# GpSimd forms the low parts of a weight tile in four operations of 256 columns instead of one of 1024

## The chip, the cores and the metric

The kernel runs on one core of one Trainium2 chip. The metric is the device time of one execution in microseconds (us). A core has TensorE (matrix products; the profile keeps its matmuls, PE, apart from its weight loads, PEld), VectorE (DVE), ScalarE (ACT), GpSimd (POOL) and SyncE (SP, which here issues DMAs).

## The reference

One encoder layer over 512 tokens of width 1024, float32:

```python
# x: (1, 512, 1024)
p = rmsnorm(x, norm1_g) @ w_in          # one combined projection
p_A, p_B, g_A, g_B = split(p)
y_A = rwkv7_bidirectional(p_A, ...)     # 8 heads of 64: a recurrence over the tokens, forwards and backwards
y_B = neighbourhood_attention_2d(p_B)   # 8 heads, tokens as an 8 x 64 grid, window of 8 x 16
x = x + (sigmoid(g_A) * (y_A @ w_oA) + sigmoid(g_B) * (y_B @ w_oB)) @ w_out
x = x + hier_moe(rmsnorm(x, norm2_g))   # 4 groups of 8 experts, top 1 group, top 2 experts in it
```

`rwkv7_bidirectional` ends in a normalisation over each head's 64 columns, and `neighbourhood_attention_2d` normalises q and k per head: both need an inverse square root for each token and head.

## The kernel before

A projection is computed in tiles of 128 output columns. The weight tile, `w_raw`, has 128 partitions by 1024 numbers: eight blocks k of 128 x 128, one for each 128 rows of the weight. TensorE multiplies rounded operands (`fp32r`), so each operand is split in two: a high part, rounded, and a low part, what is left. `proj` (L303) adds up three products for each k, low weight by high activation, high by high, and high by low, so 24 matmuls of 128x512 a tile.

`wsplit` (L294) makes the two parts of a weight tile. ScalarE writes `w_hi`, a rounded copy. Then `w_lo` = `w_raw` - `w_hi` is one subtraction over the whole tile: on VectorE for the 15 first tiles of `w_in` but one and for the later `wo` and `w_out` tiles, on GpSimd for the others of `w_in` (`m >= 15` in `proj`) and for the second tile of the kernel: 30 tiles on VectorE, 29 on GpSimd. `w_raw`, `w_hi` and `w_lo` have two buffers each. SP issues the loads of `w_raw`.

The work runs in this order. The first 15 tiles of `w_in` are RWKV's input (`rwkv_tile`). For each of two groups of heads the kernel then prepares per-chunk matrices (`prep_unit`, whose results are `T`, `KB` and the state `R`), inverts triangular blocks (`invert`: a series of small DVE operations on `pr` and `TI`, each dependent on the one before, then a 32x32 transpose into `MT`), and walks through 16 chunks one after the other (`chain_step`: products into `c`, copies to `X` and `R` by ScalarE and DVE, then the state's product with the decay `EX`, a DVE operation with PSUM input). `chain_out` normalises the result: `gx`, `gst` and `rs_i` are its small DVE operations, and `yc` is scaled by DVE for one half and by GpSimd for the other. Tiles of attention's q, k, v and of the gates (`others`) are projected in between, to fill TensorE while the chain waits; a scheduler sets the order of each engine from the dependencies and the priorities that the code gives. `na_qk` normalises q and k over `osq`; `na_block` adds the bias `BM`, formed on GpSimd, to the attention scores. From about 560 us on, the output projections and the experts follow.

Both normalisations call `rsqrt_bits`, which is a series of eleven small DVE operations, each on the result of the one before: a shift by one bit of the number's own bits (`nrs_i` in `na_qk`, `rs_i` in `chain_out`), one multiply and add on it (`nst`, `gst`), and three Newton steps of three operations.

In the profile a helper's operation has the helper's line: L188 is an activation on ScalarE, L191 a `tensor_tensor`, L194 a `scalar_tensor_tensor`, L198 and L200 a `tensor_scalar`, L203 a matmul and L206 a transpose on TensorE.

Of the kernel before, what the change touches and what calls it, by code (L numbers as in the profile page):

```python
# [8 lines left out]
F32 = mybir.dt.float32  # L9
# [4 lines left out]
OP = mybir.AluOpType  # L14
# [4 lines left out]
D = 1024  # L19
# [162 lines left out]
class K:  # L182
# [111 lines left out]
    def wsplit(self, raw, eng=None):  # L294
        hi = self.wpool.tile([P, 8, P], F32R, name="w_hi", tag="w_hi", bufs=2)
        lo = self.wpool.tile([P, 8, P], F32R, name="w_lo", tag="w_lo", bufs=2)
        self.act(hi.rearrange("p a b -> p (a b)"), raw)
        self.tt(lo.rearrange("p a b -> p (a b)"), raw, hi.rearrange("p a b -> p (a b)").bitcast(F32), OP.subtract, eng=eng)
        return hi, lo

    def wload(self, m, name="w_in", eng=None):
# [1150 lines left out]
```

## Time and profile before

| | |
|---|---|
| median of 3 runs | 927.93 us (926.7 to 929.12) |
| profiled execution | 931.2 us |
| its span on the core | 929.4 us |
| mean granted TensorE clock | 0.949 of full speed |
| TensorE matmul busy | 814.1 us, 88% of the span |
| VectorE busy | 433.4 us, 47% |
| ScalarE busy | 308.9 us, 33% |
| GpSimd busy | 181.5 us, 20%, 161 instructions |
| of this `w_lo` on GpSimd | 70.6 us, 29 tiles |

A row of the timeline gives an instruction's start in the span and its duration in us, its engine and line, the operation, the tiles (out<-in) with their shape, how many equal neighbours the row stands for, and in brackets the engine's idle time before it and what ended that. A row of a group gives the count, the busy time in us, the mean of one in ns, and the idle time before them with what ended it. A row of waits gives who waited for whom, in us, how often, and the longest.

### The profile page before, as it was taken

To read this page: it belongs to the slowest core of one execution; us is meant where nothing else is said; L and a number is where in the kernel's file an instruction comes from. 1 tells how busy PE (TensorE), PEld (TensorE's weight loads), DVE (VectorE), ACT (ScalarE), POOL (GpSimd) and SP (SyncE) were. 2 spreads that over 40 slices of the span, in tenths; PEclk is the share of its full clock that TensorE was granted. 3 is DMA by queue.
4 is the path that set the end of the run, shared out by engine and by line. 5 is a ranking of instruction groups with operands and counts; after the bars stand their busy time and mean duration, and the time that the engine had idled before them with its cause. 6 is when DMAs were issued, how large, how long until landed. Compare 5 with 4: busy or idle time off the path is not lost. (4 is left out here: it accounts for less than half of the span.)

```text
span 929.4 us, 17293 instructions
## 1 busy us (share of the span) xinstructions
PE 814.1 (88%) x7192; PEld 529.8 (57%) x7192; DVE 433.4 (47%) x870; ACT 308.9 (33%) x667; POOL 181.5 (20%) x161
## 2 busy tenths in 40 slices
PE   8999887889987987799999999999669999888784
PEld 7676555556666765566666677878533333333331
DVE  5798984565689587224436505643612111111010
ACT  6454531123433553034756722223211111111110
POOL 2611121120003142123312230003321121211010
PEclk9999996899999999599999999999779999999998
DMA  6311130212112311422224548889989999999982
GB/s 216 110 59 47 35 102 26 68 58 69 36 59 81 125 53 62 140 72 67 81 68 137 182 135 287 300 326 380 353 330 410 394 345 395 395 393 400 398 341 44
DMA packets 49263, 176.18 MB, mean 190 GB/s; under 512 B 7584, under 2 KB 14368, under 8 KB 37152
## 3 DMA queue, kind: packets, MB, share of 16 engines
q1 hardware_dynamic: 43936, 164.56, 48.1%
q0 software_dynamic: 5248, 10.50, 4.2%
q8 instruction: 57, 0.93, 0.4%
q14 instruction: 22, 0.18, 0.1%
HBM read 159.30 MB, written 24.12 MB: 197 GB/s over the span
## 5 line engine op out<-in xcount | busy, mean ns | idle before, releaser
L203 PE MATMUL G<-ws,xT 128*64 128x512 f32 x512 | 128.9, 600 | 5.1 <-DMA ws<-in_wgu 3.8
L203 PE MATMUL mm<-hT_hi,w_lo 128*128 128x512 f32 x264 | 113.9, 432 | 7.9 <-ACT oth L188 6.8
L191 POOL TENSOR_TENSOR w_lo<-w_raw,w_hi 128x1024 fp32r<-128x1024 f32 x29 | 70.6, 2436 | 237.2 <-ACT w_hi L188 213.8
L203 PE MATMUL mm<-hT_hi,w_hi 128*128 128x512 f32 x264 | 112.0, 424 | 0.0
L203 PE MATMUL mm<-hT_lo,w_hi 128*128 128x512 f32 x264 | 111.2, 421 | 0.0
L203 PEld LDWEIGHTS G<-ws,xT 128*64 128x64 f32 x512 | 44.5, 138 | 77.7 <-issue 65.3
L203 PE MATMUL Yd<-ws,hT 128*64 128x512 f32 x256 | 65.7, 606 | 9.7 <-ACT y L188 8.7
L188 ACT ACTIVATE w_hi<-w_raw 128x1024 fp32r<-128x1024 f32 x59 | 62.2, 1055 | 30.5 <-PE mm L203 29.4
L203 PEld LDWEIGHTS mm<-hT_hi,w_lo 128*128 128x128 f32 x264 | 51.9, 197 | 26.2 <-issue 15.3
L191 DVE TENSOR_TENSOR w_lo<-w_raw,w_hi 128x1024 fp32r<-128x1024 f32 x30 | 37.7, 1257 | 50.1 <-ACT w_hi L188 50.1
L203 PEld LDWEIGHTS mm<-hT_lo,w_hi 128*128 128x128 f32 x264 | 51.8, 196 | 12.7 <-issue 2.0
L203 PEld LDWEIGHTS mm<-hT_hi,w_hi 128*128 128x128 f32 x264 | 52.0, 197 | 11.3 <-issue 1.5
L191 DVE TENSOR_TENSOR sg<-sg,G 128x256 f32<-128x256 f32 x16 | 6.7, 421 | 96.9 <-ACT sg L188 96.9
L1382 POOL DMA_INDIRECT out<-y,idx x16 | 25.2, 1577 | 117.3 <-DVE y L198 100.4
L198 DVE TENSOR_SCALAR y<-Yd,wts 128x512 f32<-128x512 f32 (+1 forms) x16 | 11.7, 734 | 77.1 <-PE Yd L203 62.6
L188 ACT ACTIVATE sg<-G,wts 128x256 f32<-128x256 f32 x16 | 7.6, 474 | 118.0 <-PE G L203 118.0
L651 DVE COPY R<-c 32x128 f32<-32x128 f32 x64 | 18.7, 293 | 52.6 <-ACT R L188 52.0
L203 PE MATMUL c<-R,T 128*32 128x64 f32 (+1 forms) x992 | 36.8, 233 | 7.2 <-DVE nrs_i L194 2.2
L203 PEld LDWEIGHTS c<-R,T 128*32 128x32 f32 (+1 forms) x992 | 26.6, 126 | 26.3 <-issue 14.0
L203 PE MATMUL tp<-T,KB 64*64 64x128 f32 x512 | 35.2, 281 | 7.3 <-ACT T L188 7.1
L203 PEld LDWEIGHTS Yd<-ws,hT 128*64 128x64 f32 x256 | 16.6, 136 | 43.5 <-ACT y L188 21.6
L188 ACT ACTIVATE T<-tp 64x256 f32<-64x256 f32 x64 | 23.9, 378 | 44.6 <-DVE T L191 43.6
(313 smaller groups left out, 1474.5 us busy)
## 6 DMA issues: line engine op xcount, KB each, us to landing
ws<-in_wgu SPq DMA_DIRECT2D x64, 1024.0 KB, 21.1
ws<-in_wd SPq DMA_DIRECT2D x30, 1024.0 KB, 21.2
w_raw<-in_w_in SPq DMA_DIRECT2D x43, 512.0 KB, 3.6
d_oth<-oth SPq DMA_DIRECT2D x16, 256.0 KB, 2.0
w_raw<-in_wo SPq DMA_DIRECT2D x8, 512.0 KB, 3.9
w_raw<-in_w_out SPq DMA_DIRECT2D x8, 512.0 KB, 5.9
x_in<-in_x SPq DMA_DIRECT2D x4, 512.0 KB, 5.4
ga<-d_oth SPq DMA_DIRECT2D x8, 256.0 KB, 4.0
```

What stands on the lines that cost most here:

```text
L188: self.nc.scalar.activation(out, in_, func, **kw)
L191: (eng or self.nc.vector).tensor_tensor(out, a, b, op=op)
L198: self.nc.vector.tensor_scalar(out, a, s1, None, op0=op0)
L203: return self.nc.tensor.matmul(out, l, r, start=start, stop=stop, **kw)
L651: self.nc.vector.tensor_copy(R[u, :, blk, p2], ps[u, 2:4])
L1382: self.nc.gpsimd.indirect_dma_start(out=self.A["out"], out_offset=bass.IndirectOffsetOnAxis(ap=idx, axis=0), in_=y, in_offset=None, bounds ...
```

## The change

Where `wsplit` is given GpSimd as its engine, it now issues the subtraction as four operations of 256 columns each; piece i holds the blocks k = 2i and 2i + 1. VectorE's tiles are formed in one operation as before.

```diff
         self.act(hi.rearrange("p a b -> p (a b)"), raw)
-        self.tt(lo.rearrange("p a b -> p (a b)"), raw, hi.rearrange("p a b -> p (a b)").bitcast(F32), OP.subtract, eng=eng)
+
+        n = 1 if eng is None else 4
+        for i in range(n):
+            o = slice(i * D // n, (i + 1) * D // n)
+            self.tt(lo.rearrange("p a b -> p (a b)")[:, o], raw[:, o], hi.rearrange("p a b -> p (a b)").bitcast(F32)[:, o], OP.subtract, eng=eng)
         return hi, lo
```

The order of instructions on TensorE, VectorE, ScalarE and SP is the same with the change; line numbers below L299 are 4 higher. Two engines show a difference in their waits or rows. GpSimd's instructions at the first group's chain of steps, before (from the third of the five tiles there to the next operation of another kind):

```order
L191 TENSOR_TENSOR w_lo<-w_raw,w_hi 128x1024 [waits DMAHW6_49,PE_49,Activation_49]
L191 TENSOR_TENSOR w_lo<-w_raw,w_hi 128x1024 [waits DMAHW1_49,PE_49,Activation_49]
L191 TENSOR_TENSOR w_lo<-w_raw,w_hi 128x1024 [waits DMAHW3_49,PE_49,Activation_49]
L191 TENSOR_TENSOR kd<-kd,kd_3165 128x512 [waits DVE_49]
L477 COPY EX<-ep 128x16 [waits DVE_49,Activation_49]
```

and the same place after:

```order
L191 TENSOR_TENSOR w_lo<-w_raw,w_hi 128x256 [waits DMAHW6_49,PE_49,Activation_49]
L191 TENSOR_TENSOR w_lo<-w_raw,w_hi 128x256 x3
L191 TENSOR_TENSOR w_lo<-w_raw,w_hi 128x256 [waits DMAHW1_49,PE_49,Activation_49]
L191 TENSOR_TENSOR w_lo<-w_raw,w_hi 128x256 x3
L191 TENSOR_TENSOR w_lo<-w_raw,w_hi 128x256 [waits DMAHW3_49,PE_49,Activation_49]
L191 TENSOR_TENSOR w_lo<-w_raw,w_hi 128x256 x3
L191 TENSOR_TENSOR kd<-kd,kd_3216 128x512 [waits DVE_49]
```

Nothing stands between the four pieces of a tile, and only the first has waits (for ScalarE's `w_hi`, the load, and TensorE's last use of the buffer).

TensorE's instructions for one of these tiles in the same stretch, before (the tile's matmuls, up to the first four products of a chunk):

```order
L203 MATMUL mm<-hT_hi,w_lo 128x512 [waits Activation_49,Pool_49]
L203 MATMUL mm<-hT_hi,w_hi 128x512
L203 MATMUL mm<-hT_lo,w_hi 128x512
L203 MATMUL mm<-hT_hi,w_lo 128x512
L203 MATMUL mm<-hT_hi,w_hi 128x512
L203 MATMUL mm<-hT_lo,w_hi 128x512
L203 MATMUL mm<-hT_hi,w_lo 128x512
L203 MATMUL mm<-hT_hi,w_hi 128x512
L203 MATMUL mm<-hT_lo,w_hi 128x512
L203 MATMUL mm<-hT_hi,w_lo 128x512
L203 MATMUL c_2465<-R,T 64x64 [waits DVE_49]
```

and after:

```order
L203 MATMUL mm<-hT_hi,w_lo 128x512 [waits Activation_49,Pool_49]
L203 MATMUL mm<-hT_hi,w_hi 128x512
L203 MATMUL mm<-hT_lo,w_hi 128x512
L203 MATMUL mm<-hT_hi,w_lo 128x512
L203 MATMUL mm<-hT_hi,w_hi 128x512
L203 MATMUL mm<-hT_lo,w_hi 128x512
L203 MATMUL mm<-hT_hi,w_lo 128x512 [waits Pool_49]
L203 MATMUL mm<-hT_hi,w_hi 128x512
L203 MATMUL mm<-hT_lo,w_hi 128x512
L203 MATMUL mm<-hT_hi,w_lo 128x512
L203 MATMUL c_2516<-R,T 64x64 [waits DVE_49]
```

The matmul of k = 2 now waits for GpSimd by itself (those of k = 4 and 6, further on, do too), and the first one waits for the first piece alone. The rows of TensorE with a wait for GpSimd go from 32 to 112.

VectorE's instructions in this stretch, with the start of an inverse square root among the chain's (alike before and after but for buffer numbers and lines; those before are shown):

```order
L191 TENSOR_TENSOR R<-c_2630,EX 64x2x128 [waits PE_49]
L200 TENSOR_SCALAR ngx<-x 128x8 [waits PE_49]
L191 TENSOR_TENSOR R<-c_2630,EX 64x2x128
L685 TENSOR_SCALAR nrs_i<-ngx 128x8 [waits DVE_49]
L200 TENSOR_SCALAR nst<-nrs_i 128x8 [waits DVE_49]
L191 TENSOR_TENSOR nrs_i<-nst 128x8 [waits DVE_49]
```

Nothing moved here: the chain's `R` operations and the series of the inverse square root stand in one queue.

## The prediction

> **What bounds the kernel now.** I read the page's engine shares first, then the groups of instructions, then who waits for the tile `w_lo`, then the timeline around every DVE instruction that is much longer than its kind. First the page and the waits:
>
> ```profile
> PE 814.1 (88%) x7192; PEld 529.8 (57%) x7192; DVE 433.4 (47%) x870; ACT 308.9 (33%) x667; POOL 181.5 (20%) x161
> ...
> L191 POOL TENSOR_TENSOR w_lo<-w_raw,w_hi 128x1024 fp32r<-128x1024 f32 x29 | 70.6, 2436 | 237.2 <-ACT w_hi L188 213.8
> ...
> PEld mm L203 <- POOL w_lo L191: 0.7, 1, 0.7
> PE mm L203 <- POOL w_lo L191: 0.3, 1, 0.3
> ```
>
> TensorE carries the kernel, 814 of 929 us. GpSimd spends 70.6 us on the 29 tiles in question, 2.44 us each, and stands idle for 237 us in front of them, so it has room. The wait rows say that TensorE waits for such a tile once, for 0.3 us (0.7 on its load side). If the only effect were that a tile's first quarter is ready sooner, there would be next to nothing to win.
>
> The effect that I expect is on DVE. These rows are DVE's groups, then the timeline at one place of RWKV's chain of steps, all engines mixed:
>
> ```profile
> L200 DVE TENSOR_SCALAR nst<-nrs_i 128x8 int32<-128x8 int32 x8 | 7.0, 879 | 0.2
> L194 DVE SCALAR_TENSOR_TENSOR nst<-nrs_i,nst 128x8 f32<-128x8 f32 x24 | 4.0, 165 | 0.6
> ...
> 173.22 2.37 POOL L191 TENSOR_TENSOR w_lo<-w_raw,w_hi 128x1024 fp32r<-128x1024 f32 x1 [11.06 <-ACT w_hi L188]
> 173.26 2.35 DVE L200 TENSOR_SCALAR nst<-nrs_i 128x8 int32<-128x8 int32 x1
> 175.65 0.43 DVE L191 TENSOR_TENSOR R<-c,EX 64x256 f32<-64x256 f32 x1
> 176.87 0.43 PE L203 MATMUL c<-R,T 128*32 128x64 f32 x16 [2.17 <-DVE nrs_i L194]
> 178.31 0.43 DVE L410 COPY osq<-nst 128x512 f32<-128x512 f32 x1
> ```
>
> An operation on 128x8 numbers costs 165 ns in one group and 879 ns on average in the next; the 2.35 us at 173.26 shows why. It begins 0.04 us after GpSimd's `w_lo` and both end at 175.6. The next DVE instruction, which reads PSUM, takes its normal 0.43, and TensorE sits idle for 2.17 us until the chain's state is there. So a DVE operation that reads only SBUF and begins inside a GpSimd `w_lo` is held until that GpSimd instruction ends. The SBUF page of the Trainium skill ("SBUF — State Buffer", section "Who interferes with whom") says this: the pair of ports that both engines share is an exclusive lock, held for a whole instruction by whoever issued first. The trace agrees, 2.35 us against 0.17.
>
> **The change part by part.** It removes 29 GpSimd operations of 128x1024 and puts 116 of 128x256 in their place; VectorE's 30 tiles, and the order on every other engine, stay. The length of a piece isn't shown before, so it stands between these neighbours (a group with a mean in ns, and eight equal operations in a row):
>
> ```profile
> L191 POOL TENSOR_TENSOR r_xg<-x,g 128x512 f32<-128x512 f32 x8 | 10.3, 1286 | 91.0 <-DVE x L191 81.7 <-issue 5.9 <-DMA h<-r_xg 3.3
> 502.62 3.16 POOL L191 TENSOR_TENSOR BM<-bias,nam 128x128 f32<-128x128 f32 x8 [2.53 <-DVE rs_i L194]
> ```
>
> 128 columns are 3.16 / 8 = 0.395 us from start to start, 512 are 1.286: 0.0023 us a column, so 256 columns come to 0.395 + 128 x 0.0023 = 0.69. A tile then takes 2.77 instead of 2.44; 29 x 0.33 = 9.7 us more GpSimd work, hidden by the 237 us of idle time. Bounds: a quarter of the old one (0.61, as if a command were free) and twice the 128-column one (0.79). I take 0.69, on the line through the two.
>
> TensorE's waits: each tile gets three more semaphore waits, on the matmuls of k = 2, 4 and 6. The tightest tile is this one (the load side reaches its first use at 555.74):
>
> ```profile
> 552.48 2.39 POOL L191 TENSOR_TENSOR w_lo<-w_raw,w_hi 128x1024 fp32r<-128x1024 f32 x1 [4.24 <-ACT w_hi L188]
> 555.74 0.19 PEld L203 LDWEIGHTS mm<-hT_hi,w_lo 128*128 128x128 f32 x1
> ```
>
> The tile is ready at 554.87, 0.87 us ahead of its first use; the 0.33 us that it ends later fits into that, its first piece comes 1.7 us earlier, and the others are needed six matmuls apart. So the waits cost nothing at the price of 0.69, nor at 0.79.
>
> What does a held DVE operation gain? It is released at the end of a piece, so after 0.69 us at most and 0.35 on average. Is it let in between two pieces that are queued back to back? The eight `BM` operations answer it, beside four dependent DVE operations that begin under them (the first row is the same kind in the free):
>
> ```profile
> 501.47 0.18 DVE L194 SCALAR_TENSOR_TENSOR gst<-rs_i,gst 128x16 f32<-128x16 f32 x1
> ...
> 503.14 0.35 DVE L194 SCALAR_TENSOR_TENSOR gst<-rs_i,gst 128x16 f32<-128x16 f32 x1
> 503.52 0.36 DVE L191 TENSOR_TENSOR rs_i<-gst 128x16 f32<-128x16 f32 x1
> 503.92 0.35 DVE L194 SCALAR_TENSOR_TENSOR rs_i<-rs_i,gx 128x16 f32<-128x16 f32 x1
> 504.30 0.24 DVE L194 SCALAR_TENSOR_TENSOR gst<-rs_i,gst 128x16 f32<-128x16 f32 x1
> ```
>
> They start 0.38 to 0.40 us apart, as the `BM` do: one DVE operation gets in at each boundary, and only one. A lone held operation, or one followed by work that needs no shared port, thus gains most of its hold. A series of such operations gains little: under one long tile it costs 2.44 and then 0.2 an operation; under four pieces 2.77, with three operations let in on the way, so 2.44 - 2.77 + 3 x 0.2 = 0.27 us gained.
>
> Now place by place: the held operations, and the gap on TensorE that follows each.
>
> ```profile
> 82.78 1.24 DVE L198 TENSOR_SCALAR s<-s 128x512 f32<-128x512 f32 x1
> 96.05 1.18 DVE L198 TENSOR_SCALAR s<-s 128x512 f32<-128x512 f32 x1
> 105.66 1.09 PE L203 MATMUL tp<-T,KB 64*64 64x128 f32 x16 [2.73 <-ACT T L188]
> ...
> 133.46 2.52 DVE L191 TENSOR_TENSOR pr<-NT,TI 128x126 f32<-128x126 f32 x1
> 139.45 0.63 PE L206 MATMUL x<-cst,osq 128*128 128x128 f32 x4 [2.65 <-DVE TI L191]
> ...
> 189.05 1.81 DVE L200 TENSOR_SCALAR nst<-nrs_i 128x8 int32<-128x8 int32 x1
> 191.45 0.43 PE L203 MATMUL c<-R,T 128*32 128x64 f32 x16 [1.54 <-DVE nrs_i L191]
> 201.84 2.21 DVE L685 TENSOR_SCALAR nrs_i<-ngx 128x8 int32<-128x8 int32 x1
> ...
> 284.91 1.70 DVE L685 TENSOR_SCALAR rs_i<-gx 128x16 int32<-128x16 int32 x1
> 291.28 1.87 DVE L191 TENSOR_TENSOR rs_i<-gst 128x16 f32<-128x16 f32 x1
> 299.68 0.69 PE L206 MATMUL c<-cst,yc 128*128 128x128 f32 x2 [4.12 <-POOL yc L191]
> ...
> 329.05 2.08 DVE L194 SCALAR_TENSOR_TENSOR T<-sh_k,nkk,ep 64x496 f32<-64x496 f32 x1
> 331.50 0.68 DVE L191 TENSOR_TENSOR T<-sh_r,ep 64x512 f32<-64x512 f32 x1
> 331.93 1.09 PE L203 MATMUL tp<-T,KB 64*64 64x128 f32 x16 [1.00 <-ACT T L188]
> 344.47 2.73 DVE L191 TENSOR_TENSOR T<-sh_r,ep 64x512 f32<-64x512 f32 x1
> 350.29 1.09 PE L203 MATMUL tp<-T,KB 64*64 64x128 f32 x16 [1.57 <-ACT T L188]
> ...
> 368.93 2.39 DVE L191 TENSOR_TENSOR TI<-TI,pr 128x56 f32<-128x56 f32 x1
> 373.77 1.45 PE L203 MATMUL c<-MT,O 32*32 32x32 f32 x92 [4.80 <-DVE MT L605]
> 498.20 1.92 DVE L200 TENSOR_SCALAR gx<-gx 128x16 f32<-128x16 f32 x1
> 500.79 0.44 PE L206 MATMUL tp<-cst,s 128*128 128x128 f32 x2 [0.86 <-ACT s L188]
> ```
>
> - Preparation of the first head pair, 82.78 and 96.05: two small holds ahead of a gap that ScalarE ends. Between 0 and both holds; 0.5.
> - 133.46, series of the triangular inversion mixed with that of the inverse square root: the series price, 0.3.
> - 173.26: `nst` ends at the first boundary, 1.5 us earlier, and so does `R<-c,EX` behind it, which needs no shared port. But eight more operations of the series stand ahead of the `osq` copy at 178.31; three get in by the end of the tile at 176.0, the rest run at 0.2 each, so `osq` comes about 0.95 earlier. What follows is tied to both: 0.95 out of a gap of 2.17.
> - 189.05: the same with a hold of 1.81 and a gap of 1.54; 0.45.
> - 201.84: the first of a pure series, nine more operations of 128x8 behind it; 0.2.
> - 284.91 and 291.28: the two holds stand between 32-row transposes, which go through untouched, and DVE then runs without a pause to the `gst` that releases GpSimd's `yc`. Up to 1.0 + 1.5 of the 4.12; half of it, since a `sh_v` operation on the way waits for TensorE: 1.2.
> - 329.05 and 344.47: 2.08 and 2.73 against 0.68 unheld. ScalarE's `T` ends the gaps of 1.00 and 1.57, DVE's part is only one of two: 0.3 and 0.4.
> - 368.93: four operations of a series, then a transpose: 2.39 less three boundaries, 0.5 of the gap of 4.80.
> - 498.20: lone, then a reciprocal and ScalarE; the hold of 1.7 shrinks by 1.2 and the gap is 0.86: 0.7.
>
> The sum is 0.5 + 0.3 + 0.95 + 0.45 + 0.2 + 1.2 + 0.7 + 0.5 + 0.7 = 5.5 us. The profiled execution took 931.2, its span 929.4, so it would go to 925.7. The median of the runs, 927.93, is 3.3 lower, and the same 5.5 gives 922.4. What is late next at these places: ScalarE's copies of the state, the transposes, and the `R` copies.
>
> Bounds of the sum. Above: every hold vanishes to its own 0.17 and the gap behind it closes: 1.6 + 2.2 + 2.17 + 1.54 + 3.3 + 1.00 + 1.57 + 2.2 + 0.86 = 16.4, so 911.5. Below: every place behaves as a series with pieces of 0.79, 2.44 - 3.16 + 0.6 = -0.12 at each of the twelve above (173.26 with them), so 929.4.
>
> **The rivals.** First, more is won: DVE gets two operations in at a boundary, or the chain's next step depends on the released `R` alone. The 0.43 of `R<-c,EX` right behind a held operation speaks for it, the even spacing under `BM` against it. 173 and 189 would then give 3.7 instead of 1.4, and 284 to 299 and 368 together 4.2 instead of 1.7: 10.3 in all, 917.6.
>
> Second, no change: the lock isn't given up between two operations that GpSimd has queued, so that the four pieces act as one; or the series behind each hold eat what the first operation wins. The `BM` rows speak against the first, the 0.27 of a series speaks for the second. That gives 927.5, give or take 1.
>
> Third, slower: the piece is dearer than its neighbours say. A series breaks even at 4p = 2.44 + 0.6, p = 0.76 us; beyond that each of its operations waits for a piece. With p = 1.0 the series at 133, 173, 189, 201 and 368 lose 0.96 each, 4.8, and the other places still win about 1.9: 930.8. Against it stand 0.61 to 0.79 from the rows. A rule in the Trainium skill ("GPSIMD Engine Reference", section 7, "Performance pitfalls for Q7 kernels") points that way: small read commands cost about 102 cycles each and don't overlap; by its 1.2 GHz, an estimate from that page, six more of them cost 0.51 us a tile, so p = 0.74, a series gains 0.1 instead of 0.27, and the sum would be about 0.17 x 5 = 0.9 smaller, 4.6. The spacing of `BM`, where each operation has both its reads within 0.395 us, leaves room for that and decides nothing more.
>
> **How the numbers follow.** About 0.3%, 2.8 us, is what a measurement of this kernel can tell from no change: above 930.7 is slower, under 925.1 faster. Forecast 0.54 (its own range 919 to 925), the larger gain 0.16, no change in either form 0.23, slower 0.07. So faster 0.70, same 0.23, slower 0.07. The range leaves out half of the slower case, a slice of no change's upper end and the part of the larger gain beyond 13.4 of 16.4 us: 914.5 to 929.
>
> **What would show it.** In the changed trace: 116 GpSimd `w_lo` operations of 128x256, near 0.69 us from start to start; the group `nst<-nrs_i` of L200 with a mean under 0.5 us instead of 879 ns, and no 128x8 operation over 1 us; the gap in front of `c<-R,T` near 176.9 down from 2.17 to about 1; the gap behind `yc` down from 4.12 to about 3; TensorE's waits for `w_lo` not above 1 us in all. I am wrong if held operations still end only with a tile's fourth piece, if the pieces are spaced beyond 0.76, or if the holds shrink while the same gaps on TensorE stay and are ended by the operation after next.

## The result, and the profile after

The changed kernel takes 914.96 us (median of 4 runs, 911.69 to 918.23) against 928.52 for the kernel before, run beside it: a ratio of 0.9837, 95% interval 0.9805 to 0.987. That is 12 to 18 us, where 5.5 were forecast. The profiled execution took 916.96 us, its span 915.2.

From the page of the changed kernel, the engine shares and the group of the pieces:

```profile
PE 809.7 (88%) x7192; PEld 526.2 (57%) x7192; DVE 419.5 (46%) x870; ACT 309.4 (34%) x667; POOL 199.4 (22%) x248
...
L191 POOL TENSOR_TENSOR w_lo<-w_raw,w_hi 128x256 fp32r<-128x256 f32 x116 | 88.7, 796 | 225.0 <-ACT w_hi L188 225.0
```

GpSimd works 18 us longer, where the prediction has 9.7, and TensorE no longer waits for any of its tiles. VectorE, whose 870 instructions are the same, is busy for 13.9 us less: that time was not work, it was waiting inside instructions. Two of its groups, of the changed kernel:

```profile
L200 DVE TENSOR_SCALAR nst<-nrs_i 128x8 int32<-128x8 int32 x8 | 3.7, 467 | 0.2
...
L194 DVE SCALAR_TENSOR_TENSOR nst<-nrs_i,nst 128x8 f32<-128x8 f32 x24 | 4.9, 206 | 0.6
```

The first falls from 879 to 467 ns. The second rises from 165 to 206: a series that used to be held once at its head now meets several pieces. The same place in the chain of steps as in the prediction, from the timeline after (all engines):

```profile
169.98 2.80 POOL L191 TENSOR_TENSOR w_lo<-w_raw,w_hi 128x256 fp32r<-128x256 f32 x4 [10.61 <-ACT w_hi L188]
170.02 0.72 DVE L200 TENSOR_SCALAR nst<-nrs_i 128x8 int32<-128x8 int32 x1
170.78 0.43 DVE L191 TENSOR_TENSOR R<-c,EX 64x256 f32<-64x256 f32 x1
171.23 0.20 DVE L191 TENSOR_TENSOR nrs_i<-nst 128x8 f32<-128x8 f32 x1
171.47 0.42 DVE L191 TENSOR_TENSOR R<-c,EX 64x256 f32<-64x256 f32 x1
172.03 0.43 PE L203 MATMUL c<-R,T 128*32 128x64 f32 x16 [0.58 <-DVE R L191]
174.11 0.43 DVE L414 COPY osq<-nst 128x512 f32<-128x512 f32 x1
```

`nst` is held for one piece, 0.72 instead of 2.35 us, both `R` follow, and TensorE's gap is 0.58 instead of 2.17. The tile begins 3.24 us earlier than before and the `osq` copy 4.20, so `osq` gains 0.96, as forecast; TensorE gains more, because it does not wait for it. Two later gaps, from TensorE's timeline after:

```profile
291.15 0.66 PE L206 MATMUL c<-cst,yc 128*128 128x128 f32 x4 [1.98 <-POOL yc L191]
...
361.63 0.59 PE L203 MATMUL c<-MT,O 32*32 32x32 f32 x28 [2.74 <-DVE MT L609]
```

They were 4.12 and 4.80.

The place that the prediction does not name is the start. VectorE's and GpSimd's rows of the kernel before, and the TensorE row that waits:

```profile
19.34 2.39 POOL L191 TENSOR_TENSOR w_lo<-w_raw,w_hi 128x1024 fp32r<-128x1024 f32 x1 [2.81 <-ACT w_hi L188]
19.57 2.19 DVE L191 TENSOR_TENSOR c<-pv 128x15 f32<-128x15 f32 x1
21.80 3.81 POOL L363 COPY T<-id 64x2048 f32<-64x2048 f32 x2
21.91 1.87 DVE L198 TENSOR_SCALAR nkk<-pv 128x4 f32<-128x4 f32 x1
23.69 2.21 DVE L198 TENSOR_SCALAR hb<-pv 128x8 f32<-128x8 f32 x3
27.12 1.75 DVE L191 TENSOR_TENSOR w_lo<-w_raw,w_hi 128x1024 fp32r<-128x1024 f32 x1
28.93 0.50 PE L203 MATMUL x<-hT_hi,w_lo 128*128 128x512 f32 x1 [1.36 <-DVE w_lo L191]
```

and after:

```profile
18.71 2.84 POOL L191 TENSOR_TENSOR w_lo<-w_raw,w_hi 128x256 fp32r<-128x256 f32 x4 [2.81 <-ACT w_hi L188]
18.95 0.54 DVE L191 TENSOR_TENSOR c<-pv 128x15 f32<-128x15 f32 x1
19.41 0.16 DVE L198 TENSOR_SCALAR ka<-pv 128x4 f32<-128x4 f32 x1
19.48 0.71 DVE L200 TENSOR_SCALAR ka<-pv 128x4 f32<-128x4 f32 x1
20.10 0.16 DVE L200 TENSOR_SCALAR c<-c 128x15 f32<-128x15 f32 x1
20.18 0.71 DVE L198 TENSOR_SCALAR nkk<-pv 128x4 f32<-128x4 f32 x1
20.80 0.86 DVE L198 TENSOR_SCALAR hb<-pv 128x8 f32<-128x8 f32 x3
21.62 4.73 POOL L367 COPY T<-id 64x2048 f32<-64x2048 f32 x2
23.15 1.43 DVE L191 TENSOR_TENSOR w_lo<-w_raw,w_hi 128x1024 fp32r<-128x1024 f32 x1
26.17 0.39 PE L203 MATMUL x<-hT_hi,w_lo 128*128 128x512 f32 x1
```

Before, `c` is held by the whole tile, and what stands behind it then falls under GpSimd's long copies into `T` and is held a second and a third time. After, VectorE's operations slip through between the pieces, two at a time, and are done when the copies begin. VectorE's own `w_lo` comes 4 us earlier (3.3 of them gained here, since GpSimd's tile itself begins 0.6 earlier), and TensorE's gap of 1.36 is gone.

### The profile page after: what moved, and what is told of

It reads as the page before. It is cut to its first block, busy times and chain, and to the rows that moved or that the text cites. A ratio compares the mean times of both kernels' runs of the same rounds, so it can differ in the third digit from the quotient of the medians.

```text
span 915.2 us, 17391 instructions
## 1 busy us (share of the span) xinstructions
PE 809.7 (88%) x7192; PEld 526.2 (57%) x7192; DVE 419.5 (46%) x870; ACT 309.4 (34%) x667; POOL 199.4 (22%) x248
## 5 line engine op out<-in xcount | busy, mean ns | idle before, releaser
L191 POOL TENSOR_TENSOR w_lo<-w_raw,w_hi 128x256 fp32r<-128x256 f32 x116 | 88.7, 796 | 225.0 <-ACT w_hi L188 225.0
```

What stands on the lines that cost most here:

```text
L191: (eng or self.nc.vector).tensor_tensor(out, a, b, op=op)
```

## The experiments

Ratios are against the kernel before, run on the same chip.

| run | time, us | before, us | ratio (95%) |
|---|---|---|---|
| four pieces, reversed | 918.56 | 930.72 | 0.9865 (0.984 to 0.9889) |
| two pieces | 925.07 | 930.72 | 0.9933 (0.9911 to 0.9955) |
| eight pieces | 913.54 | 930.72 | 0.983 (0.9798 to 0.9862) |
| start tile alone | 928.23 | 930.72 | 0.9979 (0.9956 to 1.0003) |
| all but the start tile | 917.95 | 930.93 | 0.9853 (0.9817 to 0.9889) |
| GpSimd fills, reads nothing | 903.91 | 930.93 | 0.9729 (0.9682 to 0.9776) |
| eight pieces, copies into T split | 917.66 | 930.93 | 0.984 (0.98 to 0.9881) |
| sixteen pieces | 916.52 | 930.93 | 0.9852 (0.9815 to 0.9889) |
| all tiles on VectorE | 903.34 | 931.13 | 0.9709 (0.968 to 0.9738) |
| all on VectorE, four pieces | 909.01 | 931.13 | 0.9782 (0.9753 to 0.9811) |

Except where said, TensorE's, VectorE's and ScalarE's instructions keep the order of the kernel before.

**Lock, or an earlier first piece?**

```diff
-        for i in range(n):
+        for i in reversed(range(n)):
```

> The four pieces are issued from the last columns to the first, so that TensorE's first matmul of a tile waits for the whole tile as before, and only the boundaries between GpSimd's operations are left of the change. Lock theory (VectorE's held operations are let in at the boundaries): the time stays at that of the change, 913 to 917 us, VectorE's nst group of L200 stays near 470 ns, and TensorE's gap before c<-R,T near 172 us stays under 1 us. Early-piece theory (what counts is that the first quarter is ready sooner): back to 926 to 929 us.

The time, 918.56 us, is 1.6 above what the lock theory gave and 7 below the other; the ratio is 0.9865, its interval overlaps that of the change, and `nst` of L200 has a mean of 470 ns. TensorE's timeline of this run, at the start and in the chain:

```profile
21.64 0.50 PE L203 MATMUL mm<-hT_hi,w_lo 128*128 128x512 f32 x1 [0.73 <-POOL w_lo L191]
...
172.76 0.43 PE L203 MATMUL c<-R,T 128*32 128x64 f32 x16 [0.60 <-DVE R L191]
```

The chain's gap closes as with the change. The first row is what the earlier piece is worth: TensorE waits for the whole first tile, and of the 2.2 us that the change gains between 20.7 and 29.3 us, 1.2 are left. So about 1 us belongs to the early piece, at one place, and the rest of the gain does not need it.

**How many boundaries?** Two, eight and sixteen pieces, `n` being the only edit:

```diff
-        n = 1 if eng is None else 4
+        n = 1 if eng is None else 2      # 8, 16
```

> Two pieces of 512 columns instead of four. They should be about 1.3 us from start to start. Lock theory: a hold ends after 1.3 us at most and one boundary stands inside a tile instead of three, so about half to two thirds of the gain of 13.6 us: 918 to 922. Early-piece theory: the first half is ready 1.1 us earlier and nearly the whole gain is there, 914 to 916.

> Eight pieces of 128 columns, about 0.40 us from start to start, 3.2 us a tile. Lock theory: holds of 0.2 us on average, seven boundaries a tile: a little faster than with four, 910 to 915. Theory that the sum of GpSimd's time counts (3.2 us a tile instead of 2.8, TensorE waits for late tiles): slower than with four, 917 to 921.

> Sixteen pieces of 64 columns, about 0.26 us apart by the spacings of 512, 256 and 128 columns (1.29, 0.70, 0.40), 4.1 us a tile. Lock theory alone: holds of 0.13 us, ratio 0.978 to 0.982. With GpSimd's longer tile (a series then meets a busy port for 4.1 us, TensorE's tightest tile is 0.9 us late): no better than four or worse, 0.983 to 0.990.

From the pages of two, eight and sixteen pieces, in this order:

```profile
PE 812.2 (88%) x7192; PEld 528.3 (57%) x7192; DVE 426.2 (46%) x870; ACT 309.1 (33%) x667; POOL 187.9 (20%) x190
```

```profile
PE 809.2 (89%) x7192; PEld 525.4 (58%) x7192; DVE 415.0 (46%) x870; ACT 309.5 (34%) x667; POOL 221.4 (24%) x364
```

```profile
PE 806.8 (88%) x7192; PEld 523.1 (57%) x7192; DVE 408.1 (45%) x870; ACT 309.5 (34%) x667; POOL 259.2 (28%) x596
```

VectorE's busy time falls with each halving: 433.4, 426.2, 419.5, 415.0, 408.1. GpSimd's rises: 181.5, 187.9, 199.4, 221.4, 259.2. With two pieces the time gains 0.67% of the change's 1.63%, two fifths and less than expected (925.07 us for 918 to 922); between four, eight and sixteen it cannot be told apart. Two pieces rule out that readiness makes the gain, since the first half is then ready 1.1 us earlier. The hold itself follows the piece: `nst` at the chain's place (173.26 in the kernel before) takes 2.35, 1.28, 0.72, 0.44 and 0.31 us with one, two, four, eight and sixteen pieces. With sixteen a tile takes 4.57 us (16 x 0.286) and TensorE's load side waits 2.6 us for GpSimd's tiles, where it waited 0.7 in the kernel before; the 11 us that VectorE saves beyond four pieces bring nothing.

**Place by place.** Only the first tile split, and all but the first:

```diff
-    def wsplit(self, raw, eng=None):
+    def wsplit(self, raw, eng=None, n=1):      # n=4 and 1 at the start for the complement
...
-        self.w0.append(self.wsplit(w0[1], nc.gpsimd))
+        self.w0.append(self.wsplit(w0[1], nc.gpsimd, 4))
```

> Only GpSimd's first tile (the second of the kernel, at 19 us) is split, the other 28 are whole. If VectorE's small operations slip through between its pieces, ahead of GpSimd's long copies into T, VectorE's own w_lo comes earlier and TensorE's gap of 1.36 us before 28.9 us goes: 2 us less than before, 925 to 927, and TensorE stands 2 us ahead from 28 us on. If the 2 us at the start of the profiled run were chance (a load that landed earlier): 928 and no lead.

> The complement of the run with the start alone: GpSimd's first tile is whole, its other 28 tiles are in four pieces. If the places add up: the gain of the change less 2.2 us, so 12 to 13 us under before, a ratio near 0.987; TensorE gains nothing up to 100 us, about 3 us between 156 and 207 us, and 2 us at the yc gap near 299 us. If the lead at the start only shifts which later work is held (places that interact), the ratio is that of the whole change, 0.984, or over 0.990.

The kernel before and the changed one were also profiled once more each.

> The kernel before, profiled a second time. If the 2.8 us that the first pair of profiles differ by after 550 us belong to the change, this one takes about 366.7 us from the first output projection to the end, as the first did; if they are chance, it takes 364 to 365.

> The changed kernel, profiled a second time. If the difference after 550 us belongs to the change: 363.9 us again from the first output projection to the end; if it is chance, anything from 363.5 to 366.5. The first 100 us should again stand about 2.2 us ahead from 29 us on, whatever the loads do before that.

The table shows by how much TensorE gets ahead of the first profile of before in a stretch (the start of the same TensorE instruction in both profiles, subtracted; stretches by before's time, us):

| stretch | second profile of before | start alone | change | change, again | reversed | all but start |
|---|---|---|---|---|---|---|
| 20.7 to 29.3 | 0.0 | 2.2 | 2.2 | 2.2 | 1.2 | -0.1 |
| 160.1 to 176.9 | 0.0 | 0.0 | 1.6 | 1.8 | 1.8 | 1.2 |
| 181.8 to 207.1 | 0.1 | 0.0 | 0.8 | 0.8 | 0.8 | 0.8 |
| 290.1 to 299.9 | 0.0 | 0.0 | 2.2 | 2.2 | 2.2 | 2.2 |
| 306.1 to 350.3 | 0.0 | 0.0 | 0.7 | 0.5 | 0.5 | -0.2 |
| 350.3 to 378.3 | -0.2 | -0.3 | 1.1 | 0.5 | 1.3 | 1.5 |
| 450.1 to 525.1 | 0.3 | -0.2 | -0.6 | -0.5 | -0.5 | -0.2 |
| first output projection to the end | 1.3 | 1.6 | 2.8 | 2.7 | 2.1 | 1.9 |

The start alone gains 2.2 us there and nothing in the other places of the table; in the runs its 2.5 us are not clear of noise (the interval ends at 1.0003). Its complement has the rest, with a gain in the runs (13 us, 0.9853) that with the start's 2 adds up to that of the change within the intervals. The last line is not the change's with any certainty: that stretch took 366.7 and 365.4 us in the two profiles of before, 363.9 and 364.0 in those of the change, and 363.9 to 367.6 in the other kernels: 363.9 with eight pieces, 366.3 with eight pieces and the copies into `T` split (further down).

**Which of GpSimd's work holds VectorE?** GpSimd's low parts are zeros here, written without reading:

```diff
+        l = lo.rearrange("p a b -> p (a b)")
+        o = slice(0, D) if eng is None else slice(0, 8)
+        self.tt(l[:, o], raw[:, o], ..., OP.subtract, eng=eng)
+        if eng is not None:
+            eng.memset(l.bitcast(F32), 0.0)
```

> GpSimd subtracts 8 columns of a tile and then fills all 1024 with zeros, so its long operation reads nothing from SBUF (the low parts of its 29 tiles are left out of the result; from the first chain on the order on TensorE differs somewhat). Lock theory, with the lock on reads: no VectorE operation is held beside it, the nst group of L200 falls to 170 ns, and the time is under that of eight pieces, 905 to 913 us. If a hold needs only a busy GpSimd, the nst group stays above 400 ns and the time near 915 to 928.

903.91 us, a little less than a lock on reads was expected to give; but `nst` of L200 stays at 532 ns, which a lock on reads alone excludes. VectorE's groups, and the timelines of VectorE and GpSimd in this run:

```profile
L200 DVE TENSOR_SCALAR nst<-nrs_i 128x8 int32<-128x8 int32 x8 | 4.3, 532 | 0.2
L191 DVE TENSOR_TENSOR nrs_i<-nst 128x8 f32<-128x8 f32 x24 | 4.0, 165 | 0.7
```

```profile
152.89 0.95 POOL L303 MEMSET w_lo<- 128x1024 f32 x1
152.89 0.17 DVE L191 TENSOR_TENSOR nrs_i<-nst 128x8 f32<-128x8 f32 x1
153.09 0.17 DVE L194 SCALAR_TENSOR_TENSOR nrs_i<-nrs_i,ngx 128x8 f32<-128x8 f32 x1
...
188.15 0.96 POOL L303 MEMSET w_lo<- 128x1024 f32 x1
188.24 0.89 DVE L200 TENSOR_SCALAR nst<-nrs_i 128x8 int32<-128x8 int32 x1
```

Beside a fill, operations with two inputs run at 0.17 each, and `tensor_scalar` with one input is held to its end. So there are two holds: two-input operations wait for GpSimd's reads, one-input `tensor_scalar` for its writes too. The Trainium skill ("SBUF — State Buffer", section "Who interferes with whom") says as much: two inputs contend with an operation that reads SBUF, not with one that only writes it, while the modes that `tensor_scalar` can enter take the shared pair of ports. The fill is also shorter (0.95 us) and the order of TensorE differs from the first chain on, so the 27 us under before are no clean price of the lock.

**Other ways round it.** Eight pieces and GpSimd's copies into `T` split into four parts each:

```diff
-                nc.gpsimd.tensor_copy(self.T[sr, :, d, blk, :, 64:], id64[...].to_broadcast([64, NCH, 2, 64]))
+                for c in range(0, NCH, 4):
+                    nc.gpsimd.tensor_copy(self.T[sr, c:c + 4, d, blk, :, 64:], id64[...].to_broadcast([64, 4, 2, 64]))
```

> Eight pieces a tile, and GpSimd's four long copies into T at the start in four parts each. Lock theory: VectorE's operations at 20 to 30 us are let in there too, 0.5 to 1.5 us off eight pieces: ratio about 0.982. If TensorE bounds that stretch, no difference from eight pieces, 0.983.

The runs can't tell it from eight pieces, nor could they show 0.5 to 1.5 us; the profiles show no difference at the start: TensorE gains 2.2 us between 20.7 and 29.3 in both. Then no tile on GpSimd at all, whole and in four operations (the order differs on all engines):

```diff
-        hi, lo = self.w0.pop(0) if self.w0 else self.wload(m, eng=self.nc.gpsimd if m >= 15 else None)
+        hi, lo = self.w0.pop(0) if self.w0 else self.wload(m, eng=None)
```

> All 59 tiles' low parts on VectorE, whole; GpSimd forms none (the order of all engines differs from the first chain on). No lock is left, but each of the 29 tiles takes 1.2 us of VectorE's queue, 35 us in all, where the change holds VectorE for about 19. If only the time that VectorE loses counts: a smaller gain than the change's, 916 to 922. If VectorE has room outside the chains (46% busy): 908 to 915.

> All tiles on VectorE, each in four operations of 256 columns, so that the small operations of the chains can be ordered in between. A quarter should take about 0.33 us. If the 1.2 us pieces were what hurt in VectorE's queue: 1 to 4 us faster than whole tiles on VectorE. If not: the same, or 1 to 2 us slower for the added fixed cost of three more operations a tile (about 0.05 us each, 9 us over 59 tiles).

903.34 us, faster than both kernels and below either expectation. Its page and VectorE's group:

```profile
PE 806.8 (89%) x7192; PEld 525.6 (58%) x7192; DVE 435.3 (48%) x899; ACT 309.1 (34%) x667; POOL 112.2 (12%) x132
...
L191 DVE TENSOR_TENSOR w_lo<-w_raw,w_hi 128x1024 fp32r<-128x1024 f32 x59 | 73.4, 1244 | 39.7 <-ACT w_hi L188 39.6
```

VectorE took over 29 tiles, 29 x 1.24 = 36 us, and is busy for 435.3 us: 1.9 more than in the kernel before. By this sum, what it had lost to holds beside GpSimd's tiles was nearly as long as the work that GpSimd took from it. How much of the 27.8 us gained is due to the other order is not shown. Four operations a tile are slower (0.9782): the tiles then cost VectorE 93.6 us instead of 73.4, 20 us more where 9 were expected.

## Why the prediction was wrong, point by point

**Right.** The mechanism: VectorE's SBUF-only operations are held by GpSimd's tile and let in between the pieces; the early piece counts for little; the waits cost TensorE nothing; the pieces are 0.705 us apart in undisturbed tiles (2.82 / 4; 0.69 forecast), so no series became slower by them. Over all 29 a tile takes 3.06 us (88.7 / 29) for 2.77 forecast. The longest, 4.55 at 334.47, runs among VectorE operations of about 1 us each; that GpSimd is held there in its turn is likely, but no run tests it.

**Wrong: the sum, 5.5 us for a measured 13.6** (medians). It left out a place, it sized the holds that precede TensorE's gaps too small, and it took TensorE's matmuls as equally long before and after. In the order of its terms:

- The list of places left out the start altogether. The 2.19 us of `c` at 19.57 are as long as most holds in the list. Price: 2.2 us, shown by splitting that tile alone. A hold released there also escapes the next long GpSimd operation; the prediction prices only the hold itself.
- "One DVE operation gets in at each boundary, and only one" holds for dependent operations. Where two independent ones follow each other, two get in. VectorE's timeline of the changed kernel, the inversion mixed with the inverse square root, then a pure series:

```profile
129.92 0.85 DVE L191 TENSOR_TENSOR pr<-NT,TI 128x126 f32<-128x126 f32 x1
130.70 0.70 DVE L200 TENSOR_SCALAR nst<-nrs_i 128x8 int32<-128x8 int32 x1
131.32 0.28 DVE L191 TENSOR_TENSOR TI<-TI,pr 128x126 f32<-128x126 f32 x1
131.52 0.70 DVE L191 TENSOR_TENSOR nrs_i<-nst 128x8 f32<-128x8 f32 x1
...
157.43 0.58 DVE L200 TENSOR_SCALAR nst<-nrs_i 128x8 int32<-128x8 int32 x1
158.05 0.65 DVE L191 TENSOR_TENSOR nrs_i<-nst 128x8 f32<-128x8 f32 x1
158.74 0.66 DVE L194 SCALAR_TENSOR_TENSOR nrs_i<-nrs_i,ngx 128x8 f32<-128x8 f32 x1
```

  The first four go in pairs, one short and one held per piece; the last three go one per piece. The rows under `BM` were four dependent operations, and the rule was drawn too wide.
- 173.26, 189.05 and 201.84 were sized at 0.95 + 0.45 + 0.2 = 1.6, since "what follows is tied to both" the chain's `R` and the series that ends in `osq`. TensorE's next chain product waited for `R` alone: 1.6 to 1.8 up to 176.9 in the two profiles of the change and that of the reversed pieces (1.2 in all but the start), and 0.8 from 181.8 to 207.1, so 2.4 or more.
- 284.91 and 291.28: 1.2, "half of it, since a `sh_v` operation on the way waits for TensorE". All of it came: 2.2 in four profiles, near the 2.5 that the two holds allow.
- 329.05 and 344.47: 0.7 forecast, 0.5 to 0.7 measured with the whole change. 368.93: 0.5 forecast; 0.5 to 1.5.
- 498.20: 0.7 forecast, nothing kept. The gap of 0.86 closed and others took its place, from TensorE's timeline after:

```profile
490.29 0.48 PE L203 MATMUL x<-kT,qT 64*128 64x128 f32 x2 [0.84 <-DVE s L191]
...
513.71 0.47 PE L203 MATMUL mm<-hT_hi,w_lo 128*128 128x512 f32 x1 [0.78 <-ACT oth L188]
```

- 82.78, 96.05 and 133.46 can't be judged by start times: between 29 and 160 us the two profiles of before differ by 1.6 us and those of the change by 0.9. TensorE's idle time alone is steadier. Between 82 and 105 us it falls by 0.5 to 0.7 in the four profiles with the later tiles in four pieces and by 0.0 in the other two (0.5 forecast); between 129 and 142 by 0.1 to 0.9 in the four (0.3 forecast).

The places in the table of the changed kernel's profile come to about 2.2 + 1.6 + 0.8 + 2.2 + 0.7 + 1.1 - 0.6 = 8.0 us. The rest has another source, which the sum has no term for: TensorE's matmuls take less time with the change. A row of stretches gives a stretch, its length, then busy time and count of PE, PEld, DVE, ACT and POOL, the granted clock, and the DMA's share and rate. Here are the stretches up to the first output projection, in the two profiles of before and then the two of the change:

```profile
0.00:562.73 562.73, 498.94 (x5730) 363.15 (x5730) 341.54 (x701) 241.16 (x550) 122.73 (x111) 0.94 0.28 88
0.00:562.10 562.10, 497.93 (x5729) 362.23 (x5730) 340.65 (x701) 241.03 (x550) 122.77 (x111) 0.95 0.28 88
0.00:551.31 551.31, 494.90 (x5729) 359.95 (x5730) 327.85 (x701) 241.60 (x550) 140.70 (x198) 0.95 0.28 90
0.00:551.62 551.62, 493.36 (x5730) 359.03 (x5730) 328.37 (x701) 241.23 (x550) 140.75 (x198) 0.95 0.29 90
```

By the means of two profiles each, the stretch is 10.9 us shorter: 6.6 us are idle time of TensorE, which is what the prediction's 5.5 adds up, and 4.3 us are the same matmuls being busy for less. Hardly any of these 4.3 (0.3 of 4.0 in the first pair) lie in the places of the table; they are most of what start times show elsewhere. Of the idle time that the places gain, 1 to 2 us come back in other stretches. The granted clock differs too: it is 0.949 and 0.952 in the profiles of before, 0.956 and 0.958 with the change. In the runs it is 0.954 on average before (39 runs beside the experiments), 0.9615 with the change (4), 0.957 to 0.961 in the other kernels that have GpSimd's tiles in four pieces or more, 0.954 with the start alone and 0.955 with two pieces. Among the runs of before alone a higher clock goes with a shorter time: 932.45 to 933.5 us at 0.949, 926.44 at 0.959, 923.13 at 0.960. Whether fewer waits of TensorE raise its clock, or something else does, no run separates. After the first output projection come 2.1 us more, and what these belong to stays open.

The rival of "more is won" had the mechanism nearer, two operations at a boundary, and `R` alone as what the chain waits for; its 10.3 us still lacked the start and the matmuls' own time.

## What to carry to other kernels

An operation in the profile that takes many times the mean of its like, and ends with an instruction of the engine that shares its ports, is a wait that no wait column shows; list all of these by size, from the first microsecond on, before pricing any. Cutting the long GpSimd operation into pieces of 0.4 to 0.7 us gained 1.6 to 1.7% here. Ask first, though, whether the offloading pays at all: here VectorE had lost nearly as much time to holds as the 29 tiles cost it, and without them on GpSimd, in another order, the kernel was 2.9% faster than before. And before a difference of start times is put down to a closed wait, split it into TensorE's idle time and its matmuls' busy time.

## What the runs showed of the hardware

GpSimd's fill, which reads nothing, lets two-input VectorE operations through (165 ns) and holds one-input `tensor_scalar` (0.89 us at 188.24). GpSimd's spacing per piece was 0.705 us for 256 columns, 0.424 for 128 (3.39 / 8) and 0.286 for 64 (4.57 / 16), so a piece costs about 0.14 us beside its columns.
